# Moving the z product of a hybrid decoder layer ahead of attention, decays and the GLA preparation

## The chip, the cores and the metric

One core of one Trainium2 chip runs the whole kernel. The metric is the device time of one execution in microseconds. The runs before gave a median of 1007.89 us, from 1005.3 to 1011.02.

## What is computed

One decoder layer for 1024 tokens of width 1024, in float32. The normalized input h goes through one wide projection; its columns feed three branches, whose outputs are merged by gates and projected again.

```
h    = rms_norm(x) ; proj = h @ w_in -> aq ak av ag | gq gk gv gg gdown | sxbc sdt sz | mg
A: q,k = rope(rms_norm(aq)), rope(rms_norm(ak)); window of 128, sinks; y_a = attn(q,k,av) * silu(ag)
B: log_alpha = log_sigmoid(gdown @ w_gate_up + b) / 16, chunks of 64, cumulated inside a chunk
   y_b = rms_norm(gla(gq, gk, gv, log_alpha)) * silu(gg)
C: x,b,c = silu(causal_conv(sxbc)); dt = softplus(sdt + bias); y = ssd(x, dt, a, b, c) + D x
   y_c = group_rms_norm(y * silu(sz))
out  = x + (sum over branches of sigmoid(mg_n) * (y_n @ w_branch_n)) @ w_out
```

## The kernel before

Every large product is made of matmuls on fp32r operands, and each operand is split into a high and a low part (`wh`, `wl` for weights, `h_hi`, `h_lo` for h). `split` (L244) does it for weights: one engine rounds (ScalarE or GpSimd), another subtracts (VectorE or GpSimd), and three matmuls take the place of one. The split weights live in the pool tag `w2`, ten buffers of 128x512, which nearly all products share; raw weights come in through three buffers (`wraw`). Of the eight accumulation banks four belong to the dense products (`psd1`), four to everything else (`psm`, tag `m`).

The products with tokens on partitions are the k/v block (`kv_tiles`), two query chunks of 256 columns (`dense_tm`, called with C_Q and C_Q+1), z (`dense_pair_tm` with C_SZ) and the GLA values (C_GV). z and the values use Strassen's scheme, seven products p1 to p7 in place of eight, on sums of blocks of h: `t1`, `t2`, `t3` (`block_sums`, L487) and `t4n` (L746), all made on VectorE with help from GpSimd and ScalarE. The products with columns on partitions (`pair_fm`) use the same scheme: convolutions (`conv_pair`), merge gates (`merge_gates`), GLA q and k (`gla_pair`), branch gates `ag` and `gg`.

Written order: normalization and transposed h; k/v and first query chunk, with the rotary angles (`rope`) in between; block sums; the decays of SSD (`dz` to `acsT`, L503 to L536); the GLA preparation (L539 to L602: a small product, log-sigmoid, a cumulated sum made of 32 scans of 63 or 64 elements, and exponentials stored to `eq_d`); second query chunk; attention in eight blocks of 128 tokens; `t4n`; z; values; gates and convolutions; SSD in eight blocks; `gla_pair` and GLA in eight blocks; remaining gates; branch products (`gated`, L1054); output product.

This order is a priority and not the order of execution: when the program is built, a list scheduler with a simulated timeline fixes an order for each engine and each DMA queue, taking the instruction first in the text among those that are ready. On the chip every engine then runs its list in that fixed order. Pools are memory: a pool that is opened later may take the addresses of one that was closed before, and its first writers wait for the last users of those addresses. `glp` (GLA preparation), `att` (attention), `ssd` and `gla` follow one another in this way.

Of the kernel before, what the change touches and what calls it, by code (L numbers as in the profile page):

```python
# [26 lines left out]
NST, NW2, NHF = 4, 10, 2  # L27
# [54 lines left out]
def kernel(  # L82
# [175 lines left out]
    def dense_tm(c, evac, between=None, halves=(0, 1)):  # L258
        parts = []
        for kh in range(2):  # L260
            raw = wq.pop(0) if wq else load_w(w_tm[2 * c + kh], D, f"tm{c}_{kh}")
            parts += [split(raw[:, i * 512 : (i + 1) * 512], 512, f"tm{c}_{kh}_{i}") for i in range(2)]
        for hf in halves:
            for jj in range(2):
# [77 lines left out]
    def dense_pair_tm(c, evac, name):  # L342
# [835 lines left out]
```

## Time and profile before

| | us |
|---|---|
| median of 3 runs | 1007.89 |
| lowest and highest run | 1005.3, 1011.02 |
| profiled execution | 1011.36 |
| its span, first to last instruction | 1009.5 |
| TensorE (PE) busy | 952.8 (94%) |
| VectorE (DVE) busy | 753.0 (75%) |
| GpSimd (POOL) busy | 504.2 (50%) |
| ScalarE (ACT) busy | 446.3 (44%) |

The profile is of one execution; its times are in microseconds from the first instruction. Matmuls are pipelined and overlap in the records, so that the distance from start to start, not the length of one, is what a matmul costs. An idle time is put down to what released it. The granted clock is TensorE's, as a share of 2.4 GHz.

### The profile page before, as it was taken

What the parts mean: (1) busy time and instruction counts of PE and PEld (TensorE: products, weight loads), DVE (VectorE), ACT (ScalarE), POOL (GpSimd) and SP (SyncE); (2) the same over time, 40 slices, a digit from 0 to 9 for tenths busy, and PEclk for the clock granted to TensorE, in tenths of its full rate; (3) what the DMA queues carried; (4) which work ended last, traced back from release to release, by engine and by line L of the source; (5) the groups of instructions that cost most, each with busy time, mean ns of one, the idle gap of its engine ahead of it and who ended that gap; (6) DMA issues with size and microseconds to landing.
All of it is one profiled execution on the core that took longest, in us unless ns stands there. A gap on an engine that the chain in (4) does not pass through costs nothing.

```text
span 1009.5 us, 14874 instructions
## 1 busy us (share of the span) xinstructions
PE 952.8 (94%) x5089; PEld 804.3 (80%) x5089; DVE 753.0 (75%) x1245; ACT 446.3 (44%) x1002; POOL 504.2 (50%) x453
## 2 busy tenths in 40 slices
PE   7987879999999999999999999999899989997998
PEld 7987868898778778877888888887688878885786
DVE  4999799688799998887777554766757754589644
ACT  5433444555566467654555434444334311133221
POOL 8743557665664553344657544353344000256776
PEclk8997879899999999999999999999999999999999
DMA  9402135232324232346665444336544866763443
GB/s 370 150 32 75 54 107 183 70 120 85 110 79 129 76 118 76 116 156 212 210 181 179 136 149 135 122 119 211 187 153 173 270 211 202 247 213 107 165 148 114
DMA packets 84410, 150.14 MB, mean 149 GB/s; under 512 B 7328, under 2 KB 40304, under 8 KB 84336
## 3 DMA queue, kind: packets, MB, share of 16 engines
q1 hardware_dynamic: 84160, 149.18, 44.6%
q8 instruction: 40, 0.66, 0.3%
q14 instruction: 34, 0.28, 0.1%
q10 hardware_dynamic: 176, 0.02, 0.0%
HBM read 101.96 MB, written 47.22 MB: 148 GB/s over the span
## 4 chain that ended last, share of the span: by engine, by line
PE 53%; DVE 20%; issue 8%; DMA 7%; POOL 6%; ACT 4%; POOLq 0%; SPq 0%; DVEq 0%; ACTq 0%
PE ps_p_mg L286 16%; PE ps_u L1065 7%; PE ps_p_cv L286 5%; PE ps_p_o L286 5%; PE ps_p_gg L286 3%; PE ps_p_gqk L286 2%; PE ps_p_ag L286 2%; PE ps_tm L273 2%; PE ppv L726 1%; PE ps_kv L423 1%; DMA ybg_d<-ggy 1%; DMA e<-acs_dram 1%; PE pT L716 1%; PE ps_p_gv L369 1%; DMA el<-eq_d 1%
## 5 line engine op out<-in xcount | busy, mean ns | idle before, releaser
L286 PE MATMUL ps_p_mg<-ht_hi,wl_p_mg 128*128 128x512 f32 x192 | 75.5, 394 | 0.7 <-DVE wl_p_mg L251 0.7
L286 PE MATMUL ps_p_mg<-ht_hi,wh_p_mg 128*128 128x512 f32 x192 | 76.2, 397 | 0.0
L286 PE MATMUL ps_p_mg<-ht_lo,wh_p_mg 128*128 128x512 f32 x192 | 75.8, 395 | 0.0
L306 DVE TENSOR_TENSOR c_mg<-ps_p_mg,c_mg 128x512 f32<-128x512 f32 x84 | 56.4, 682 | 12.2 <-PE ps_p_mg L286 11.0
L251 POOL TENSOR_TENSOR wl_u<-wr_u,wh_u 128x512 fp32r<-128x512 f32 x8 | 10.6, 1328 | 100.8 <-ACT wh_u L248 100.7
L286 PE MATMUL ps_p_mg<-h_hi,wh_p_mg 128*128 128x512 f32 x144 | 56.9, 395 | 0.0
L286 PE MATMUL ps_p_mg<-h_lo,wh_p_mg 128*128 128x512 f32 x144 | 56.8, 395 | 0.0
L286 PE MATMUL ps_p_mg<-h_hi,wl_p_mg 128*128 128x512 f32 x144 | 56.5, 394 | 0.0
L251 POOL TENSOR_TENSOR wl_p_mg<-s_mg,wh_p_mg 128x512 fp32r<-128x512 f32 x24 | 31.8, 1325 | 41.4 <-ACT wh_p_mg L248 40.9
L1068 DVE SCALAR_TENSOR_TENSOR tg<-tg,ps_u 128x512 f32<-128x512 f32 x48 | 31.8, 680 | 24.9 <-DMA tg<-tg_d 22.1
L248 ACT CAST wh_p_mg<-s_mg 128x512 fp32r<-128x512 f32 x48 | 29.5, 615 | 46.7 <-POOL s_mg L298 23.6
L786 DVE SCALAR_TENSOR_TENSOR acc<-c_cv,cwh,acc 128x512 f32<-128x512 f32 (+3 forms) x48 | 40.0, 856 | 4.2 <-ACT acc L783 4.1
L286 PEld LDWEIGHTS ps_p_mg<-ht_hi,wl_p_mg 128*128 128x128 f32 x192 | 36.1, 188 | 8.2 <-DVE wl_p_mg L251 1.2
L286 PEld LDWEIGHTS ps_p_mg<-ht_hi,wh_p_mg 128*128 128x128 f32 x192 | 36.1, 188 | 7.2
L286 PEld LDWEIGHTS ps_p_mg<-ht_lo,wh_p_mg 128*128 128x128 f32 x192 | 36.1, 188 | 7.0
L251 DVE TENSOR_TENSOR wl_p_mg<-wr_mg,wh_p_mg 128x512 fp32r<-128x512 f32 x36 | 29.9, 832 | 14.3 <-PE ps_p_mg L286 6.1
L701 ACT ACTIVATE sc<-sc,nm 128x256 f32<-128x256 f32 (+1 forms) x64 | 30.8, 483 | 21.9 <-DVE nm L696 21.9
L273 PE MATMUL ps_tm<-wh_tm,h_hi 128*128 128x256 f32 x128 | 36.8, 289 | 3.9 <-ACT spl L433 3.9
L248 ACT CAST wh_u<-wr_u 128x512 fp32r<-128x512 f32 x24 | 14.9, 621 | 57.8 <-PE ps_u L1065 49.1
L308 DVE SCALAR_TENSOR_TENSOR c_o<-ps_p_o,c_o 128x512 f32<-128x512 f32 x28 | 18.9, 688 | 27.9 <-POOL c_o L312 17.6
L273 PE MATMUL ps_tm<-wl_tm,h_hi 128*128 128x256 f32 x128 | 36.3, 292 | 0.3 <-DVE wl_tm L251 0.3
L273 PE MATMUL ps_tm<-wh_tm,h_lo 128*128 128x256 f32 x128 | 36.5, 287 | 0.0
(470 smaller groups left out, 3452.2 us busy)
## 6 DMA issues: line engine op xcount, KB each, us to landing
wr_mg<-in_w_fm_dram SPq DMA_DIRECT2D x24, 512.0 KB, 3.6
tg_d<-c_mg SPq DMA_DIRECT2D x24, 512.0 KB, 2.6
tg<-tg_d SPq DMA_DIRECT2D x24, 512.0 KB, 4.4
wr_u<-in_w_br_dram SPq DMA_DIRECT2D x24, 256.0 KB, 3.5
xq<-in_xf_dram SPq DMA_DIRECT2D x8, 512.0 KB, 10.8
wr_cv<-in_w_fm_dram SPq DMA_DIRECT2D x8, 512.0 KB, 3.6
xbc_d<-acc SPq DMA_DIRECT2D x16, 256.0 KB, 2.5
e<-acs_dram SPq DMA_DIRECT2D x16, 256.0 KB, 4.9
```

The lines of the kernel that those rows point to most:

```text
L248: A.copy(hi[:, :n], raw)
L251: (lo_eng or V).tensor_tensor(out=lo[:, :n], in0=raw, in1=hi[:, :n].bitcast(F32), op=ALU.subtract)
L273: T.matmul(ps[:, j, :], lhsT=l, rhs=w, start=n == 0, stop=n == 23)
L286: T.matmul(ps, lhsT=l[:, k, :], rhs=r, start=n == 0, stop=n == 3 * kt - 1)
L306: V.tensor_tensor(out=o, in0=p, in1=c, op=op)
L308: V.scalar_tensor_tensor(out=o, in0=p, scalar=scale, in1=c, op0=ALU.mult, op1=op)
L369: T.matmul(ps[:, 256 * j : 256 * j + 256], lhsT=l, rhs=r, start=n == 0, stop=n == 11)
L423: T.matmul(ps[:, :N_KV], lhsT=l, rhs=w[:, k, :], start=n == 0, stop=n == 23)
L701: A.activation(out=sc[:, j, :nk], in_=sc[:, j, :nk], func=AF.Exp, bias=nm[:, h : h + 1], accum_out=dn[:, h : h + 1])
L786: V.scalar_tensor_tensor(out=acc[:, z:], in0=r[:, o + z - d : o + 512 - d], scalar=cwh[:, 4 * c + 3 - d : 4 * c + 4 - d], in1=acc[:, z:], ...
L1065: T.matmul(ps, lhsT=l[:, k, :], rhs=r, start=m_ == 0, stop=m_ == 11)
L1068: V.scalar_tensor_tensor(out=o, in0=o, scalar=1.0, in1=ps, op0=ALU.add, op1=ALU.mult)
```

## The change

The head: the root of a token tile's mean square goes ahead of the scaling of x by the norm's weights on GpSimd, and for the first two tiles VectorE does this scaling together with that by the root, eight times 128x128 in place of twice 128x512. Two of the four k/v weight splits change from GpSimd to VectorE or back. The high parts of the first query chunk's weights are made on ScalarE and not on GpSimd.

The second query chunk comes directly behind the first one and runs over the contraction index first (`dense_tm_by_k`): its eight token tiles accumulate side by side in the four `m` banks, and it holds only the weights of the step at hand. Its copies out come at the end.

The rotary angles go behind the block sums. `t4n` and z come next, and z's split weights get a pool of twelve buffers, `zp`, which is closed behind z; attention's pools are opened behind that. Then come the decays, whose small tiles now lie in one `w2` buffer, and attention.

The GLA preparation goes behind the last convolution, ahead of SSD. Its data is kept in an order with the halves of all chunks together, so that 4 scans of 511 or 512 elements with a row of ones and zeros that starts them anew take the place of 32; ScalarE's ReLU takes the place of VectorE's minimum; the step behind the scans is done in halves. One pair of merge gates goes ahead of `gla_pair(0)` and one ahead of `gla_pair(1)`.

```diff
--- before.py
+++ after.py
@@
-NST, NW2, NHF = 4, 10, 2
+NST, NW2, NHF, NZ = 4, 10, 2, 12
...
+    root = {}
+
     def stats(a, b):
         for t in range(a, b):
             A.activation(out=xr[t], in_=xr[t], func=AF.Square, accum_out=ssx[:, t : t + 1])
+        root[a] = rsqrt(const, rstd[:, a:b], ssx[:, a:b], b - a, 1.0 / D, EPS, f"x{a}")
+        for t in range(max(a, 2), b):
             for i in range(2):
                 hs = slice(4 * i, 4 * i + 4)
-                G.tensor_tensor(out=xs[t][:, hs], in0=xs[t][:, hs], in1=ngk[:, hs].unsqueeze(2).to_broadcast([P, 4, P]), op=ALU.mult)
-        rsqrt(const, rstd[:, a:b], ssx[:, a:b], b - a, 1.0 / D, EPS, f"x{a}")
+                with tc.issue_after(root[a].ins):
+                    G.tensor_tensor(out=xs[t][:, hs], in0=xs[t][:, hs], in1=ngk[:, hs].unsqueeze(2).to_broadcast([P, 4, P]), op=ALU.mult)
 
     def transposed(t):
         pt = mtile(f"rT{t}")
@@ -222,7 +226,11 @@
         sl = slice((t % 4) * P, (t % 4 + 1) * P)
         for kh in range(2):
             xk = xs[t][:, 4 * kh : 4 * kh + 4]
-            V.tensor_tensor(out=xk, in0=xk, in1=pt[:, :P].unsqueeze(1).to_broadcast([P, 4, P]), op=ALU.mult)
+            if t >= 2:
+                V.tensor_tensor(out=xk, in0=xk, in1=pt[:, :P].unsqueeze(1).to_broadcast([P, 4, P]), op=ALU.mult)
+            else:
+                for k in range(4 * kh, 4 * kh + 4):
+                    V.scalar_tensor_tensor(out=xs[t][:, k], in0=xs[t][:, k], scalar=ngk[:, k : k + 1], in1=pt[:, :P], op0=ALU.mult, op1=ALU.mult)
             hi, lo = (p[:, :, sl] for p in hb["12"[kh] + "12"[t // 4]])
             A.copy(hi, xk)
             V.tensor_tensor(out=lo, in0=xk, in1=hi.bitcast(F32), op=ALU.subtract)
@@ -230,9 +238,13 @@
     def split_kv(i):
         sl = slice(2 * i, 2 * i + 2)
         A.copy(wkh[:, sl], wkr[:, sl])
-        (V if i == 3 else G).tensor_tensor(out=wkl[:, sl], in0=wkr[:, sl], in1=wkh[:, sl].bitcast(F32), op=ALU.subtract)
-
-    for a in "s01 t0 w0 w1 s12 t1 w2 w3 s23 t2 s34 t3 s46 t4 t5 s68 t6 t7".split():
+        if i < 2:
+            V.tensor_tensor(out=wkl[:, sl], in0=wkr[:, sl], in1=wkh[:, sl].bitcast(F32), op=ALU.subtract)
+        else:
+            with tc.issue_after(root[1].ins):
+                G.tensor_tensor(out=wkl[:, sl], in0=wkr[:, sl], in1=wkh[:, sl].bitcast(F32), op=ALU.subtract)
+
+    for a in "s01 t0 w0 w1 s12 w2 w3 t1 s23 t2 s34 t3 s46 t4 t5 s68 t6 t7".split():
...
@@
-    def split(raw, n, name, act=False, lo_eng=None):
-        hi = wpool.tile([P, 512], F32R, tag="w2", bufs=NW2, name=f"wh_{name}")
-        lo = wpool.tile([P, 512], F32R, tag="w2", bufs=NW2, name=f"wl_{name}")
+    def work(dt, name):
+        return wpool.tile([P, 512], dt, tag="w2", bufs=NW2, name=name)
+
+    def split(raw, n, name, act=False, lo_eng=None, work=work):
+        hi, lo = work(F32R, f"wh_{name}"), work(F32R, f"wl_{name}")
...
@@
-            parts += [split(raw[:, i * 512 : (i + 1) * 512], 512, f"tm{c}_{kh}_{i}") for i in range(2)]
+            parts += [split(raw[:, i * 512 : (i + 1) * 512], 512, f"tm{c}_{kh}_{i}", act=c == C_Q) for i in range(2)]
...
@@
+    def dense_tm_by_k(c, evac):
+
+
+        raws = [load_w(w_tm[2 * c + kh], D, f"tm{c}_{kh}") for kh in range(2)]
+        banks = [psm.tile([P, 2, 256], F32, tag="m", name=f"ps_tm{c}_{b}") for b in range(4)]
+        for q in range(4):
+            parts = [p.rearrange("p (k c) -> p k c", c=256) for p in split(raws[q // 2][:, (q % 2) * 512 : (q % 2) * 512 + 512], 512, f"tm{c}_{q}", True)]
+            for k in (2 * q, 2 * q + 1):
+                hi, lo = (p[:, k % 2, :] for p in parts)
+                for b in range(4):
+                    for j in range(2):
+                        sl = slice((2 * (b % 2) + j) * P, (2 * (b % 2) + j + 1) * P)
+                        l_hi, l_lo = (r[:, sl] for r in rows_of(k, b // 2))
+                        for i, (l, w) in enumerate(((l_hi, hi), (l_lo, hi), (l_hi, lo))):
+
+                            T.matmul(banks[b][:, j, :], lhsT=l, rhs=w, start=k == 0 and i == 0 and j == 0, stop=k == KT - 1 and i == 2,
+                                     skip_group_check=True)
+        for b in range(4):
+            evac(b // 2, b % 2, banks[b])
...
@@
-    dense_tm(C_Q, spill_tm(qkv_d, 0), lambda i: [kv_tiles(q) for q in KVO[i + 1]] + ([rope()] if i == 2 else []))
+    dense_tm(C_Q, spill_tm(qkv_d, 0), lambda i: [kv_tiles(q) for q in KVO[i + 1]])
     kvp_scope.close()
+    dense_tm_by_k(C_Q + 1, spill_tm(qkv_d, 256))
...
@@
+    posf = const.tile([P, NT], F32, name="posf")
+    V.tensor_copy(posf, posi)
+    ra, rb = (st_tile(f"rope{i}", (P, 4, NT, 32)) for i in range(2))
+    ang, a2, pr, rr, fs = ra[:, 0], ra[:, 1], ra[:, 2], ra[:, 3], rb[:, 0]
...
+    hb["t4n"] = (big_tile(F32R, "ht4_hi"), big_tile(F32R, "ht4_lo"))
+    with tc.high_priority():
+        for k in range(4):
+            f1, f2 = half_tile(f"fc{k}"), half_tile(f"fd{k}")
+            whole(f1, "t2", k, G)
+            whole(f2, "21", k, V)
+            block_diff(f1, f2, f1, "t4n", k)
+
+    def z_block(col, tok, blk):
+        for i in range(2):
+            th = half_tile(f"zth{col}{tok}{i}")
+            A.activation(out=th, in_=blk[i], func=AF.Tanh, scale=0.5)
+            V.scalar_tensor_tensor(out=blk[i], in0=th, scalar=1.0, in1=blk[i], op0=ALU.add, op1=ALU.mult)
+        store_tm(z_d, col, tok, blk)
+
+    with tc.tile_pool(name="zp", bufs=NZ) as zp:
+        dense_pair_tm(C_SZ, z_block, "z", lambda dt, nm: zp.tile([P, 512], dt, tag="z2", name=nm))
...
-    with tc.tile_pool(name="smp", bufs=1) as smp:
-        dz = smp.tile([P, NT, 8], F32, name="dz")
...
+    sd = wpool.tile([P, 512], F32, tag="w2", bufs=NW2, name="sd")
+    dz, da, de, dw, dl = (sd[:, 64 * i : 64 * i + 64].rearrange("p (t h) -> p t h", h=8) for i in range(5))
+    ah, acsT = sd[:, 320:328], sd[:64, 384:512]
...
-    with tc.tile_pool(name="glp", bufs=1) as gp:
...
-            for t in range(NT):
-                o = t * P
-                V.tensor_tensor_scan(out=mn[:, f, o : o + 63][:, ::-1], data0=ones.to_broadcast([P, 63]), data1=la[:, f, o + 1 : o + 64][:, ::-1],
-                                     initial=0.0, op0=ALU.mult, op1=ALU.subtract)
-                V.tensor_tensor_scan(out=mn[:, f, o + 64 : o + P], data0=ones.to_broadcast([P, 64]), data1=la[:, f, o + 64 : o + P],
-                                     initial=0.0, op0=ALU.mult, op1=ALU.add)
...
-    dense_tm(C_Q + 1, spill_tm(qkv_d, 256))
...
-    dense_pair_tm(C_SZ, z_block, "z")
...
@@
     conv_pair(2)
+
+
+    eq_d = dram.tile([2, 2, P, S], F32, name="eq_d")
+    bmid = dcyp.tile([P, 2, NT], F32, name="bmid")
+    cst = dcyp.tile([P, 2, NT], F32, name="cst")
+    with tc.tile_pool(name="glp", bufs=1) as gp:
...
+        keep = gp.tile([P, 512], F32, name="keep")
+        G.memset(keep, 1.0)
+        G.memset(keep.rearrange("p (t l) -> p t l", l=64)[:, :, 0:1], 0.0)
...
+                A.activation(out=by_half(la, f)[:, :, ts], in_=pv, func=AF.Abs, bias=gb)
+                A.activation(out=by_half(mn, f)[:, :, ts], in_=pv, func=AF.Relu, scale=-1.0, bias=ngb[:, f : f + 1])
...
+            V.tensor_tensor_scan(out=mn[:, f, 0:511][:, ::-1], data0=keep[:, 0:511], data1=la[:, f, 1:512][:, ::-1],
+                                 initial=0.0, op0=ALU.mult, op1=ALU.subtract)
+            V.tensor_tensor_scan(out=mn[:, f, 512:S], data0=keep, data1=la[:, f, 512:S], initial=0.0, op0=ALU.mult, op1=ALU.add)
+            bv, lv = by_half(mn, f), by_half(la, f)
+            V.memset(bv[:, 0, :, 63], 0.0)
+            for h in range(2):
+                V.scalar_tensor_tensor(out=bv[:, h], in0=iot[:, 64 * h : 64 * h + 64].unsqueeze(1).to_broadcast([P, NT, 64]), scalar=av, in1=bv[:, h], op0=ALU.mult, op1=ALU.add)
+            V.scalar_tensor_tensor(out=bmid[:, f, :], in0=lv[:, 0, :, 0], scalar=av, in1=bv[:, 0, :, 0], op0=ALU.add, op1=ALU.subtract)
+            V.tensor_copy(cst[:, f, :], bv[:, 1, :, 63])
+            for i, ex in enumerate((la[:, f], eb)):
+                A.activation(out=ex.rearrange("p (t h l) -> p h t l", h=2, l=64), in_=bv, func=AF.Exp, scale=(1.0 if i == 0 else -1.0) / 16)
+                Q.dma_start(eq_d[i, f], ex)
...
@@
+    merge_gates(0, U_MGA, 0)
     gla_pair(0)
-    merge_gates(0, U_MGA, 0)
-
+    merge_gates(0, U_MGA, 2)
     gla_pair(1)
...
@@
-    merge_gates(0, U_MGA, 2)
     merge_gates(0, U_MGA, 4)
     merge_gates(0, U_MGA, 6)
```

## Rows read from the trace of the kernel before

**Rows 1.** Stages: width; busy (count) PE, PEld, DVE, ACT, POOL; clock, DMA, GB/s.

```profile
12.00:28.50 16.50, 12.27 (x55) 11.48 (x56) 11.67 (x15) 6.20 (x12) 15.58 (x18) 0.69 1.02 407
...
71.50:109.00 37.50, 26.80 (x203) 26.08 (x204) 29.55 (x59) 21.10 (x31) 8.25 (x9) 0.86 0.20 65
109.00:171.50 62.50, 48.87 (x348) 46.86 (x348) 59.87 (x100) 24.64 (x41) 43.18 (x37) 0.86 0.33 112
171.50:228.00 56.50, 53.31 (x422) 51.27 (x421) 43.58 (x98) 29.49 (x82) 36.36 (x37) 0.94 0.35 111
228.00:440.00 212.00, 209.67 (x1074) 165.07 (x1073) 188.70 (x376) 127.89 (x305) 105.25 (x96) 1.00 0.29 93
...
593.00:686.00 93.00, 93.00 (x500) 76.67 (x499) 52.11 (x82) 42.44 (x128) 40.85 (x44) 1.00 0.43 142
```

**Rows 2.** Timeline of TensorE, first query chunk: start, length, engine, line.

```profile
44.09 0.28 PE L273 MATMUL ps_tm<-wh_tm,h_hi 128*128 128x256 f32 x1
44.21 0.28 PE L273 MATMUL ps_tm<-wh_tm,h_lo 128*128 128x256 f32 x1
```

**Rows 3.** Waits of TensorE, 71.5 to 228 us: total, times, longest.

```profile
PE pacs L528 <- DVE da L526: 6.4, 1, 6.4
PE ps_p_z L369 <- ACT wh_p_z L248: 6.2, 3, 4.6
PE ps_tm L273 <- ACT spl L433: 3.9, 1, 3.9
PE ps_p_z L369 <- DVE wl_p_z L251: 3.7, 1, 3.7
```

**Rows 4.** Groups of VectorE, 92.5 to 145 us: busy us, mean ns, idle before.

```profile
L590 DVE TENSOR_TENSOR_SCAN mn<-ones,la 128x64 f32<-128x64 f32 x16 | 7.4, 462 | 0.0
L588 DVE TENSOR_TENSOR_SCAN mn<-ones,la 128x63 f32<-128x63 f32 x16 | 7.3, 459 | 0.0
L582 DVE SCALAR_TENSOR_TENSOR la<-mn,la 128x1024 f32<-128x1024 f32 x2 | 4.5, 2285 | 5.2 <-ACT la L580 5.2
...
L585 DVE TENSOR_SCALAR la<-la,avr 128x1024 f32<-128x1024 f32 x2 | 2.8, 1424 | 0.0
```

**Rows 5.** Timelines: VectorE's first step of the GLA preparation; SP's issues.

```profile
93.38 1.28 DVE L556 COPY gd<-gdT 16x512 f32<-16x512 f32 x2 [0.64 <-DMA acs_dram<-acsT]
...
140.53 0.32 SPq L600 DMA_DIRECT2D eq_d<-mn  x1
143.71 0.32 SPq L620 DMA_DIRECT2D qk<-qkv_d  x1
```

**Rows 6.** Timeline of TensorE: ends and starts along the chain.

```profile
438.77 1.09 PE L726 MATMUL ppv<-pT,vv 128*64 128x256 f32 x8
...
463.74 0.66 PE L849 MATMUL px<-ident,xin 128*128 128x128 f32 x4 [1.18 <-DMA xin<-xbc_d]
...
685.12 0.60 PE L939 MATMUL ybT<-ident,ug 128*128 128x128 f32 x4
...
740.74 0.39 PE L286 MATMUL ps_p_gg<-h_hi,wh_p_gg 128*128 128x512 f32 x1
740.96 0.39 PE L286 MATMUL ps_p_gg<-h_lo,wh_p_gg 128*128 128x512 f32 x1
```

**Rows 7.** Waits of TensorE, 9 to 28.5 us.

```profile
PE ps_kv L423 <- DVE h_lo L228: 2.9, 2, 1.8
PE rT L219 <- POOL rstd L129: 0.9, 1, 0.9
```

**Rows 8.** Timelines: VectorE's scans at 120 us, and GpSimd beside them.

```profile
120.47 0.25 DVE L588 TENSOR_TENSOR_SCAN mn<-ones,la 128x63 f32<-128x63 f32 x1
120.65 1.36 DVE L590 TENSOR_TENSOR_SCAN mn<-ones,la 128x64 f32<-128x64 f32 x1
...
120.57 5.05 POOL L351 TENSOR_TENSOR wr_a_z<-wr_a_z 128x512 f32<-128x512 f32 x4 [2.05 <-DMA wr_a_z<-in_w_tm_dram]
```

More of the change, by code (lines that the diff above doesn't have):

```diff
@@ L340, in dense_pair, with dense_pair_tm @@
         return c1, c2
-    def dense_pair_tm(c, evac, name):
+    def dense_pair_tm(c, evac, name, work=work):
         def load(i, nm):
@@ L356, in mul @@
         def mul(w, key, nm):
-            parts = [split(w[i], 512, f"{nm}{i}_{name}", True, G if nm in (Z_LO if c == C_SZ else GV_LO) else None) for i in range(2)]
+            parts = [split(w[i], 512, f"{nm}{i}_{name}", True, G if nm in (Z_LO if c == C_SZ else GV_LO) else None, work) for i in range(2)]
             out = []
@@ L388, in dense_pair_tm @@
         a22 = load(3, "a22")
-        s3 = combs([wpool.tile([P, 512], F32, tag="w2", bufs=NW2, name=f"s3{i}_{name}") for i in range(2)], a11, a21, ALU.subtract)
+        s3 = combs([work(F32, f"s3{i}_{name}") for i in range(2)], a11, a21, ALU.subtract)
         s1 = combs(a21, a21, a22, ALU.add)
@@ new lines, with frac @@
+    V.tensor_scalar(out=a1, in0=ang, scalar1=1.0, scalar2=0.0, op0=ALU.mult, op1=ALU.add)
+    V.tensor_tensor(out=a2, in0=ang, in1=a1.bitcast(F32), op=ALU.subtract)
+    def frac(v):
+        V.tensor_scalar(out=rr, in0=v, scalar1=MAGIC_ROUND, scalar2=MAGIC_ROUND, op0=ALU.add, op1=ALU.subtract)
+        V.tensor_tensor(out=v, in0=v, in1=rr, op=ALU.subtract)
+    first = True
+    for a, i in ((a2, 3), (a1, 4), (a2, 2), (a1, 3), (a2, 1), (a1, 2), (a2, 0), (a1, 1), (a1, 0)):
+        av = a.bitcast(F32) if a is a1 else a
+        tgt = fs if first else pr
+        V.tensor_scalar(out=tgt, in0=av, scalar1=C2PI[i], scalar2=None, op0=ALU.mult)
+        frac(tgt)
+        if a is a1 and i == 0:
+            frac(tgt)
+        if not first:
+            V.tensor_tensor(out=fs, in0=fs, in1=pr, op=ALU.add)
+        first = False
@@ new lines, with store_tm @@
+    V.tensor_scalar(out=pr, in0=fs, scalar1=0.25, scalar2=None, op0=ALU.add)
+    for v, dst in ((fs, 1), (pr, 0)):
+        frac(v)
+        V.tensor_scalar(out=v, in0=v, scalar1=0.49999997, scalar2=-0.49999997, op0=ALU.min, op1=ALU.max)
+        A.activation(out=cs[:, dst], in_=v, func=AF.Sin, scale=6.2831855)
+    z_d = dram.tile([NT, P, 512], F32, name="z_d")
+    gv_d = dram.tile([NT, P, 512], F32, name="gv_d")
+    def store_tm(dst, col, tok, blk):
+        for i in range(2):
+            t = 4 * tok + 2 * i
+            Q.dma_start(dst[t : t + 2, :, 256 * col : 256 * col + 256].rearrange("t p c -> p t c"), blk[i].rearrange("p (t c) -> p t c", c=256))
@@ new lines @@
+    hb["t4n"] = (big_tile(F32R, "ht4_hi"), big_tile(F32R, "ht4_lo"))
[6 more added lines that the diff above has]
+    def z_block(col, tok, blk):
+        for i in range(2):
+            th = half_tile(f"zth{col}{tok}{i}")
+            A.activation(out=th, in_=blk[i], func=AF.Tanh, scale=0.5)
+            V.scalar_tensor_tensor(out=blk[i], in0=th, scalar=1.0, in1=blk[i], op0=ALU.add, op1=ALU.mult)
+        store_tm(z_d, col, tok, blk)
@@ new lines @@
+    V.scalar_tensor_tensor(out=da, in0=dt_t, scalar=-1.0, in1=ah.unsqueeze(1).to_broadcast([P, NT, 8]), op0=ALU.mult, op1=ALU.mult)
+    pa = mtile("pacs")
+    T.matmul(pa[:, :64], lhsT=triu, rhs=da.rearrange("p t h -> p (t h)"), start=True, stop=True)
+    V.tensor_copy(acs_t.rearrange("p t h -> p (t h)"), pa[:, :64])
+    A.activation(out=eacs_t, in_=acs_t, func=AF.Exp)
+    V.tensor_single_scalar(out=nacs, in_=acs_t, scalar=-1.0, op=ALU.mult)
+    pb = mtile("pacsT")
+    T.transpose(pb[:64, :P], acs_t.rearrange("p t h -> p (t h)"), ident)
@@ L607 @@
+    V.tensor_copy(acsT, pb[:64, :P])
+    Q.dma_start(acs_dram, acsT)
     ya_d = dram.tile([P, 4, S], F32, name="ya_d")
```

196 lines of the change are left out of this document (63 added, 133 removed).

## Prediction

> **What bounds the kernel now.** I read the stage table first, cutting the span where the matmul stages change. From 228 us on TensorE is full: 209.67 us busy of the 212 to 440, 93.00 of the 93 from 593 to 686 [rows 1]. Little can be won there except by taking matmuls away, and the change takes none away. Ahead of 228 it is another picture. A 128x256 matmul starts every 0.12 us when nothing waits [rows 2]. The second query chunk's stage, 71.5 to 109, holds 188 such matmuls of 203 (22.6 us) and about 2.5 us of small ones, but lasts 37.5: 12.4 lost. The z stage, 109 to 171.5, holds 336 (40.3 us) and 1 us of attention, and lasts 62.5: 21 lost. The value stage, to 228, holds 336 again and about 9 us of attention in 56.5: 7 lost. That is 40 us, part of it idle time and part matmuls at half speed: the granted clock of these stages is 0.86, 0.86 and 0.94, so in some slices it fell from 2.4 to 1.2 GHz behind the idle stretches, and is 1.00 in the two later ones [rows 1].
>
> The list of waits says who is late: VectorE's `da` (the decays) 6.4 us, ScalarE's and VectorE's parts of z's weights 6.2 and 3.7, an evacuation 3.9 [rows 3]. VectorE is the engine behind all of them: in the z stage it is busy 59.87 of 62.5 us [rows 1], and what it does there is mostly not z: the gate angles (the GLA preparation), whose scans take 7.4 + 7.3 us and two passes 4.5 + 2.8 [rows 4]. So TensorE bounds the kernel, but ahead of 228 it is starved by VectorE's order of work.
>
> Behind that stands a chain which TensorE's fullness hides: attention (first load 143.7, last product 440), SSD (first transpose 463.7), GLA (last transpose 685.7), then the gg product from 740.7 on and the 269 us from there to the end [rows 5, 6]. Between GLA's end and gg lie 55 us of other matmuls, the slack of this chain.
>
> **The parts of the change.**
>
> Second query chunk by k in four banks. Before, its weights found no work buffers until the first chunk let go of eight of ten, and were queued on VectorE behind block sums, angles and decays; hence the 3.9 + 6.4 us and half clock after them. Now a step needs two buffers and has 48 matmuls (5.8 us at 0.12) of cover for the next split. Four evacuations come together at the end, but z accumulates in the other four banks, so they cost TensorE nothing; without that cover the price is that of the wait for an evacuation above, 3.9. I count 11 of the 12.4 us as won (bounds 6 and 12.4).
>
> z ahead, with twelve buffers of its own. The GLA preparation leaves this stretch: its four largest rows alone are 22.0 us of VectorE time [rows 4], of the 89.4 us that VectorE works between 71.5 and 171.5 [rows 1]. That leaves 67.4 us, in which decays, attention's first preparation and the smaller steps of the GLA preparation are still counted; these go behind z too, and the two products need 63 us of TensorE (22.6 + 40.3). So VectorE fits, not loosely: the angles of the rotary positions stay ahead of z in the text, now behind the block sums, and part of their work comes into this stretch. z's last weight block is loaded through SP behind others, and the t4n sums share two half tiles with the evacuations: I leave 6 us of loss. Gain 15 of 21 (bounds 5 and 20).
>
> The value product then starts near 133 instead of 171. It still shares VectorE with attention's preparation: 3 of 7 us (bounds 0 and 6).
>
> Head. TensorE waits 2.9 us for split rows of x and 0.9 us for a root on GpSimd [rows 7], and the clock is at 0.69 in those 16.5 us [rows 1]: idle 4.2, and up to 5.1 us of capacity in the clock. Roots now go ahead of the scalings on GpSimd, and two tiles' scalings (2 each) go into VectorE as eight 128x128 operations; none such is in the rows; the nearest are the 64-element scan at 0.25 us [rows 8] and an eighth of a 1024-element pass, at 2.285 / 8 = 0.29 for 128 elements [rows 4], so 2.0 to 2.3 us a tile in place of two products of 512, which by the same pass are 1.1 each. VectorE gains nothing, GpSimd is relieved. ScalarE, busy 6.20 of 16.5 us, takes casts from GpSimd free of charge. I take a gain of 4 (bounds 0 and 8).
>
> Sum of the gains: 11 + 15 + 3 + 4 = 33 us (bounds 11 and 46).
>
> The GLA preparation at its new place, behind the last convolution, ahead of SSD. It issues the same matmuls, 4 scans in place of 32, two halves instead of one pass, ReLU on ScalarE for a pass on VectorE, the same four 512 KB stores on SP. A scan of 512 lies between 0.25 us (fixed cost alone) and 8 x 0.25 = 2.0 (all by the element); the 1024-element passes grow with size, so nearer the upper: 1.4, four of them 5.6 for what was 14.7. VectorE time falls by some 9 us in all.
>
> TensorE has cover there: merge and gqk products, 18.5 us a pair (84 matmuls of 512 columns, one every 0.22 us [rows 6]). What is not free is the chain: the preparation's memory is what attention gives up, and SSD's is what the preparation gives up. Memory is given on like this in the trace: the last store of the angles issues at 140.53 and attention's first load only at 143.71 [rows 5], long after its data were there. So the preparation goes into the chain. It took 47 us before (93.38 to 140.53 [rows 5]) beside a full VectorE; from attention's end to SSD's first transpose there are 24 us now [rows 6]. I take 52 in place of these 24 (bounds 30, if SSD's loads and the preparation overlap, and 71, if they don't and it takes 47 again).
>
> The chain after is then: attention's start S + 296 (143.7 to 439.9) + 52 + 222 (463.7 to 685.7) + 3 + 269 = S + 842. With z's memory free at 133 to 135, 977 us. By TensorE: 1009.5 - 33 = 976.5. Two bounds that meet cost a little on either side, which I put at 2: span 979. The profiled execution's time is 1011.36 for a span of 1009.5, so 981; it was 3.5 us above the median of 1007.89. I predict 980, between 981 and the 977 that the median's basis would give. Half a per cent, 5 us, is about what a measurement here can tell from nothing.
>
> **The rivals.**
>
> A, the chain outlasts the filler. For it: both bounds stand at 977, so every microsecond of a longer preparation shows; VectorE is 188.70 of 212 us busy just ahead of its new place [rows 1], and SP carries the gates' weights behind its four stores. Against: the scans are fewer, and the merge gates don't need the chain. With 70 us in place of 52 the chain ends at 135 + 860 = 995, time 996; 988 to 1001 for 62 to 74.
>
> B, z still starves, by GpSimd. While GpSimd's weight sums ran (four in 5.05 us), a scan took 1.36 us instead of 0.25 [rows 8]: VectorE waits for it. z's own buffers let more of that work run early, beside VectorE's two-input operations. SBUF — State Buffer of the Trainium skill ("SBUF: two separate sides") says that a GpSimd operation and a VectorE operation with two SBUF inputs lock one pair of ports against each other for a whole instruction; the trace agrees, with 1.36 against 0.25. If VectorE so gives back 6 of the chunk's 12.4 us, 11 of z's 21 and none of the value stage's, the gain is 6 + 11 + 0 + 4 = 21 us: 988.5 by TensorE, and by the chain, with S 9 us later at 144, 986. Time 984 to 996.
>
> C, slower: attention gets z's memory too late. Nothing decides but S: at 167.5 the chain gives 1009.5, at 172 half a per cent more. If z ends at 171.5 as today, because the angles and the t4n sums stand ahead of it on VectorE, attention starts 28 us later than now and the chain ends at 1013.5 or above: 1013 to 1020. Against: at least 22 us of VectorE time leave the stretch ahead of that point.
>
> D, nothing to measure: the same with S from 161 to 171, 1003 to 1013.
>
> **How the numbers follow.** Forecast 0.58 (966 to 988; of it 0.03 lie below 966), A 0.17, B 0.13, C 0.06, D 0.06. The range 966 to 998 holds the forecast's 0.55, B, and four fifths of A: 0.82. Faster by over 0.5% (below 1002.9) are forecast, A and B: 0.88; same 0.06; slower 0.06. The forecast's own range is 966 to 988.
>
> **What would show it.** z's first matmul near 92 and its last near 133; no wait of TensorE above 4 us between 60 and 175, and a granted clock of 1.00 there; attention's first load at 130 to 140. The GLA stores at 455 to 480, SSD's first transpose at 470 to 485, GLA's last transpose near 700, and gg following within 20 us. Wrong would be: angles on VectorE between z's weight halves with TensorE idle (B, C), or idle TensorE between 440 and 740, where there is almost none today (A).

## The result, and the profile after

The changed kernel takes 996.1 us (median of four runs, 994.7 to 996.9) against 1008.7 for the kernel before on the same chip: ratio 0.9876, interval 0.9845 to 0.9908. On another chip it was 998.7 against 1008.4, ratio 0.9893 (0.9873 to 0.9913). So it is faster by 10 to 13 us, where the forecast was 28. The profiled execution took 995.85 us for a span of 994.1, 15.4 us less than the span before; the accounts below are made against these spans. The profiled execution before (1011.36) lies 2.7 us above its median, so the two traces show some 3 us more than the medians do.

The stage table of the changed kernel, cut where its matmul stages change: second query chunk, z, value product, rest of attention, attention's end to SSD's first transpose, SSD and GLA. Columns as in [rows 1].

```profile
64.10:92.10 28.00, 24.88 (x194) 24.47 (x193) 27.45 (x43) 12.03 (x20) 14.05 (x11) 0.94 0.24 81
92.10:147.70 55.60, 46.76 (x341) 45.72 (x339) 45.22 (x68) 17.50 (x30) 26.78 (x18) 0.88 0.28 93
147.70:201.40 53.70, 51.17 (x413) 49.51 (x412) 41.89 (x99) 23.85 (x66) 37.47 (x48) 0.97 0.33 107
201.40:442.60 241.20, 235.11 (x1199) 187.25 (x1198) 209.17 (x413) 145.59 (x342) 117.02 (x104) 0.99 0.30 100
442.60:502.70 60.10, 56.38 (x248) 45.36 (x247) 44.40 (x64) 31.15 (x47) 25.60 (x22) 1.00 0.38 130
502.70:732.00 229.30, 224.52 (x1190) 187.16 (x1191) 170.66 (x244) 113.79 (x324) 120.24 (x118) 1.00 0.54 174
```

Beside [rows 1]: up to the second chunk the kernel now needs 64.1 us instead of 71.5, the chunk 28.0 instead of 37.5, z 55.6 instead of 62.5, the value product 53.7 instead of 56.5. That is 26.6 us less. From there to the end it needs 792.7 instead of 781.5, 11.2 more. Some 4 of these are matmuls that moved behind the value product (the preparation's 12, 1.8 us by their starts, and 20 of attention's transposes, 2.0); about 7 are new loss. By the prediction's own measure (length less matmuls at 0.12 us and the small ones) the chunk still loses 5.0 us (12.4 before), z 15.2 (21), the value product some 5.5 (7).

TensorE's waits between 60 and 205 us, total, times, longest, to set beside [rows 3]:

```profile
PE ps_p_z L403 <- POOL wl_p_z L265: 3.5, 2, 2.7
PE ps_tm L308 <- ACT wh_tm L262: 2.4, 1, 2.4
PE ps_p_z L403 <- DVE ht_lo L487: 2.3, 1, 2.3
PE ps_p_z L403 <- ACT ht_hi L486: 2.0, 1, 2.0
...
PE ps_p_z L403 <- ACT c_z L418: 1.1, 1, 1.1
```

The decays' 6.4 us and the evacuation's 3.9 are gone. z's own waits add up to 8.9 us; the other 6.3 of its 15.2 go with the clock, granted at 0.88 over the stage (the 0.12 that it lacks are 6.7 of 55.6 us). What stands behind these waits, on the timelines of VectorE, ScalarE and GpSimd (`spl` is a copy of the second query chunk out of an accumulation bank; it and the t4n sums `fc` and `fd` share the two half tiles, buffers of 128x512):

```profile
103.61 0.29 DVE L534 TENSOR_SCALAR rope<-rope 128x256 f32<-128x256 f32 x1
104.97 0.69 DVE L467 COPY spl<-ps_tm 128x512 f32<-128x512 f32 x1 [1.07 <-DMA qkv_d<-spl]
107.90 1.33 DVE L481 TENSOR_TENSOR fd<-h_hi,h_lo 128x512 f32<-128x512 f32 x1 [2.25 <-DMA qkv_d<-spl]
...
102.94 0.42 ACT L535 ACTIVATE cs<-rope 128x256 f32<-128x256 f32 x1 [10.89 <-DVE rope L534]
103.27 0.57 ACT L467 COPY spl<-ps_tm 128x512 f32<-128x512 f32 x1
...
106.21 1.26 POOL L481 TENSOR_TENSOR fc<-ht_hi,ht_lo 128x512 f32<-128x512 f32 x1 [15.76 <-DMA qkv_d<-spl]
107.43 1.26 POOL L265 TENSOR_TENSOR wl_p_z<-wr_a_z,wh_p_z 128x512 fp32r<-128x512 f32 x1
```

Read from the bottom: GpSimd's `wl_p_z`, for which TensorE waits, stands behind the first t4n sum `fc`; that idled 15.76 us for a half tile, which a copy out of the second chunk (`spl`) held; and the copies stood on VectorE behind the block of rotary angles, and on ScalarE behind Sin, which waits for the same angles.

The block of angles and decays is itself drawn out. VectorE and GpSimd ahead of the stretch above:

```profile
83.66 0.21 DVE L581 TENSOR_TENSOR sd<-sd 128x64 f32<-128x64 f32 x1
83.99 1.31 DVE L582 TENSOR_TENSOR sd<-sd 128x64 f32<-128x64 f32 x1
...
83.92 5.11 POOL L385 TENSOR_TENSOR wr_a_z<-wr_a_z 128x512 f32<-128x512 f32 x4 [0.46 <-DVE sd L581]
```

Between 78 and 91 us, while GpSimd makes weight sums and halves for z, nine small operations of VectorE (four of the angles, five of the decays) take 0.90 to 1.53 us each; the same shapes take 0.20 to 0.43 where GpSimd is idle. That is some 9.5 us of the block that ends at 103.9, an estimate from these durations. This is rival B's mechanism.

The chain, answering [rows 5] and [rows 6], from timelines of SP, TensorE and VectorE:

```profile
147.75 0.33 SPq L609 DMA_DIRECT2D qk<-qkv_d  x1
...
441.54 1.09 PE L715 MATMUL ppv<-pT,vv 128*64 128x256 f32 x8
...
446.11 1.28 DVE L788 COPY eb<-gdT 16x512 f32<-16x512 f32 x2 [1.52 <-DMA ya_d<-yat]
...
491.03 0.32 SPq L842 DMA_DIRECT2D eq_d<-eb  x1
...
502.73 0.63 PE L888 MATMUL px<-ident,xin 128*128 128x128 f32 x4 [1.42 <-DMA e<-acs_dram]
...
726.54 0.39 PE L320 MATMUL ps_p_gg<-h_hi,wh_p_gg 128*128 128x512 f32 x1
...
731.30 0.60 PE L979 MATMUL ybT<-ident,ug 128*128 128x128 f32 x4
```

Attention's first load comes at 147.75, later than before (143.71); the preparation takes 45 us; SSD's first transpose comes 60 us after attention's end, where I had 52. The gg product begins 5 us ahead of GLA's last transpose. In the head, [rows 7] has given way to two waits between 9 and 28.5 us, and the clock granted from 12 to 28.5 is 1.00 instead of 0.69:

```profile
PE ps_kv L457 <- ACT h_hi L235: 1.7, 1, 1.7
PE ps_tm L287 <- ACT wh_tm L262: 0.5, 1, 0.5
```

### The profile page after: what moved, and what is told of

Same layout as the page of the kernel before. It is cut to its first block, busy times and chain, and to the rows that moved or that the text cites. A ratio compares the mean times of both kernels' runs of the same rounds, so it can differ in the third digit from the quotient of the medians.

```text
span 994.1 us, 14844 instructions
## 1 busy us (share of the span) xinstructions
PE 944.2 (95%) x5089; PEld 795.8 (80%) x5089; DVE 765.0 (77%) x1228; ACT 451.1 (45%) x1014; POOL 491.2 (49%) x442
## 4 chain that ended last, share of the span: by engine, by line
PE 40%; DVE 12%; DMA 8%; issue 7%; POOL 5%; ACT 5%; SPq 0%; POOLq 0%; DVEq 0%; ACTq 0%
PE ps_p_mg L320 14%; PE ps_p_o L320 5%; PE ps_p_ag L320 4%; PE ps_u L1104 3%; PE ps_p_cv L320 3%; DMA tg<-tg_d 2%; PE ps_p_gqk L320 2%; DVE acc L749 1%; DMA tl<-t_d 1%; DMA yc_r<-yc_d 1%; PE py L928 1%; PE ppv L715 1%; DMA yb_r<-ybg_d 1%; POOL s_o L332 1%; PE psc L677 1%
## 5 line engine op out<-in xcount | busy, mean ns | idle before, releaser
L265 POOL TENSOR_TENSOR wl_u<-wr_u,wh_u 128x512 fp32r<-128x512 f32 x8 | 10.6, 1331 | 98.6 <-ACT wh_u L262 98.5
L320 PE MATMUL ps_p_mg<-h_hi,wh_p_mg 128*128 128x512 f32 x144 | 56.5, 392 | 0.0
L265 DVE TENSOR_TENSOR wl_p_mg<-wr_mg,wh_p_mg 128x512 fp32r<-128x512 f32 x36 | 38.4, 1074 | 15.7 <-ACT wh_p_mg L262 8.9
L733 ACT ACTIVATE c_mg<-c_mg 128x1024 f32<-128x1024 f32 x24 | 25.4, 1056 | 15.3 <-DVE c_mg L340 12.5
L320 PEld LDWEIGHTS ps_p_mg<-h_lo,wh_p_mg 128*128 128x128 f32 x144 | 27.1, 188 | 5.4
L320 PEld LDWEIGHTS ps_p_mg<-h_hi,wl_p_mg 128*128 128x128 f32 x144 | 27.1, 188 | 5.3
```

Of the source, the lines that this page charges most:

```text
L265: (lo_eng or V).tensor_tensor(out=lo[:, :n], in0=raw, in1=hi[:, :n].bitcast(F32), op=ALU.subtract)
L320: T.matmul(ps, lhsT=l[:, k, :], rhs=r, start=n == 0, stop=n == 3 * kt - 1)
L733: A.activation(out=c, in_=c, func=AF.Tanh, scale=0.5)
```

## The experiments

Ratios are to the kernel before on the same chip, with 95% intervals; "z's last" is z's last matmul, "first product" attention's. Gains and losses against the changed kernel compare ratios with its two, 0.9876 and 0.9893. The expectations count 46 operations of VectorE for the angles; the traces have 48.

**1. Sin late.** The angles' results are written to `cs`, and Sin follows z's last tanh.

```diff
-        V.tensor_scalar(out=v, in0=v, ...)
-        A.activation(out=cs[:, dst], in_=v, func=AF.Sin, ...)
+        V.tensor_scalar(out=cs[:, dst], in0=v, ...)
...
+    with tc.issue_after(zlast[0].ins):
+        for dst in range(2):
+            A.activation(out=cs[:, dst], in_=cs[:, dst], func=AF.Sin, ...)
```

> After with one edit: VectorE's chain of rotary angles stays where it is and writes its clipped values into cs; the two Sin activations follow z's last tanh on ScalarE, in place on cs. Theory 1 (ScalarE's order: Sin waits 10.89 us for VectorE, and the copies out and casts behind it wait too): z's last matmul goes from 147.7 to 139 to 142 us, the time from 996.1 to 988 to 991. Theory 2 (VectorE's chain of some 46 small operations is itself what z waits for): z's last matmul stays within 2 us, the time at 994 to 998. Theory 3 (the t4n sums find only two half tiles, which the copies out of the second chunk hold): the two copies on VectorE still stand behind its chain, so at most 3 us, 993 to 996.

1000.6 us, 0.9926 (0.9902 to 0.9950), above all three forecasts; z's last 145.7. Taking away the 10.89 us that ScalarE idles brings z 2 us and the end nothing: theory 1 falls.

**2. Half tiles of their own** for the t4n sums (`fc`, `fd` from a pool of four).

> After with one edit: the t4n sums get four half tiles of their own, in a pool that lives as long as z's. Theory 3 (half tiles): GpSimd's first t4n sum moves from 106.2 us to before 92, its idle 15.76 us go, z's last matmul comes at 137 to 141, time 986 to 990. Theory 1 (ScalarE's order): the copy of z's first product still comes behind Sin at 104; z ends at 144 to 147, time 993 to 996. Theory 2 (VectorE's chain): VectorE's half of the sums still stands behind the angles, z ends at 145 to 148, time 994 to 997.

998.9 us, 0.9907 (0.9883 to 0.9931). z's last comes at 141.7, 6 us earlier, but the value product's last at 201.0 (201.4 in the changed kernel). Its waits between 60 and 201 us:

```profile
PE qT L651 <- ACT qh L647: 4.3, 1, 4.3
PE ps_tm L308 <- ACT wh_tm L262: 4.2, 1, 4.2
PE ps_p_z L403 <- DVE c_z L409: 3.1, 1, 3.1
```

The half tiles held most of z's wait, and taking it away wins nothing: TensorE, which works through its list in order, now waits for attention's first transposes, for VectorE's additions behind the angles, and for weights that GpSimd's earlier sums delay (beside them VectorE's sums take 1.78 us instead of 0.68).

**3. Angles behind z.** The whole block is issued after z's last VectorE operation.

> After with one edit: the whole block of rotary angles is ordered behind z's last VectorE operation. All three theories of z's wait want z to end earlier here, theory 2 most: z's last matmul at 133 to 138 instead of 147.7 (theory 1 and 3: 137 to 142). The angles, 46 operations at about 0.32 us, then lie ahead of attention's first rotation: attention's first product stays within 5 us of 190.7. If the chain from attention to the gates sets the end as much as TensorE does, the time stays at 993 to 998 in spite of z's gain; if only TensorE's fullness sets it, it falls to 984 to 988.

1014.5 us, 1.0053 (1.0034 to 1.0073). Its z stage and SSD's first transpose:

```profile
91.50:134.40 42.90, 40.72 (x338) 40.30 (x336) 31.49 (x35) 13.45 (x23) 19.95 (x13) 1.00 0.32 108
...
518.55 1.09 PE L892 MATMUL px<-ident,xin 128*128 128x128 f32 x4 [7.71 <-DMA bcin<-xbc_d]
```

z runs at full clock almost without loss. Attention's first product comes at 219.0, 28 us late, not within 5 as forecast, and TensorE then runs dry ahead of SSD: from 440 to 620 us it is busy for 167.0 us at a clock of 0.93 (171.5 at 1.00 in the changed kernel). When it is this late, the chain does bind.

**4. Angles early**, inside the first query chunk as in the kernel before.

> After with one edit: the angles stand where they stood in the kernel before, in the first query chunk behind its third bank. Theory 2 (VectorE is full, the angles only move the wait): z's first matmul comes 5 to 12 us later than 92.1 and the time is within 3 us of 996. Theory 1 and 3 (place in the order, not sum): z's first matmul within 3 us of 92, its last at 137 to 142, attention begins earlier by as much, time 986 to 990.

999.0 us, 0.9913 (0.9884 to 0.9943): z's first matmul of the main run at 95.0, z's last at 147.5; a wait of 5.7 us for VectorE's `wl_tm` opens in the second chunk. The wait moves and the time is within 3 us, as theory 2 has it, though z's first matmul is 3 us late and not 5 to 12.

**5. No angles.**

```diff
-    posf = const.tile([P, NT], F32, name="posf")
...
-        A.activation(out=cs[:, dst], in_=v, func=AF.Sin, scale=6.2831855)
+    G.memset(cs, 0.5)
```

> After with the rotary angles left out: cs is filled with a constant on GpSimd, the 46 VectorE operations and two Sin go. Theory A (VectorE's sum of work up to attention's first product sets z's end and attention's start together, and what it gains there reaches the end): z's last matmul at 134 to 137 us instead of 147.7, attention's first product at 176 to 182 instead of 190.7, time 980 to 986. Theory B (what z gains is given back behind it whatever VectorE does, the end being set by what comes after attention): z at 134 to 137, time 990 to 998.

988.4 us, 0.9801 (0.9770 to 0.9832). The z stage and the value stage:

```profile
93.70:135.70 42.00, 40.76 (x341) 40.55 (x339) 33.38 (x37) 15.57 (x27) 28.34 (x18) 1.00 0.38 121
135.70:192.70 57.00, 53.09 (x412) 51.45 (x411) 41.89 (x99) 23.49 (x65) 37.71 (x48) 0.91 0.31 100
```

The stage is 13.6 us shorter than in the changed kernel and z loses next to nothing (42.0 us for 40.3 of matmuls); the value stage gives back 3.3, with 3.9 us of waits for attention's first transposes and a clock of 0.91; 7.5 to 9.5 reach the end. Without the angles z's loss is gone; the size lies between both theories.

**6. Angles in the head**, where VectorE idles, with loads and buffers of their own.

> After with the angles moved to where VectorE idles (6.35 us ahead of its first weight split at 8.5, 3.46 us at 28.7): positions and row constants are loaded first on ScalarE's queue, the angles have a buffer of their own and are written behind the head, Sin follows the last cast of x. Theory A: z's last matmul at 135 to 140, attention's first product at 177 to 184; the head loses 2 to 4 us; time 983 to 990. Theory B: 992 to 998. If the idle time of the head is not usable, the kv product starts later by up to 10 us and the time is 994 to 1001.

1005.7 us, 0.9974 (0.9955 to 0.9992), above all three forecasts. VectorE and GpSimd around the start of its z product (window 92 to 120, then GpSimd's timeline):

```profile
92.00:120.00 28.00, 24.52 (x197) 24.32 (x197) 7.74 (x13) 9.73 (x17) 15.87 (x13) 0.95 0.17 57
...
97.02 2.63 POOL L300 TENSOR_TENSOR wl_p_z<-wr_a_z,wh_p_z 128x512 fp32r<-128x512 f32 x2 [18.50 <-ACT wh_p_z L297]
...
114.89 1.26 POOL L516 TENSOR_TENSOR fc<-ht_hi,ht_lo 128x512 f32<-128x512 f32 x1 [5.52 <-DMA qkv_d<-spl]
```

The head and the first chunk end 6 us later. VectorE is busy 7.74 of 28 us and z still takes 53.5: ScalarE casts weights late and copies out behind them, and the half tiles are late again. The same wait has another engine behind it, so an idle VectorE alone is not enough.

**7. GLA preparation ahead of attention** (its new form, behind z and the decays).

> After with the GLA preparation (in its new form) put back ahead of attention, behind z and the decays. From attention's end to SSD's first transpose: 20 to 35 us instead of 60. Theory A: VectorE's sum ahead of attention grows by the preparation, attention's first product comes 20 to 35 us later than 190.7, and the time is 1005 to 1018. Theory B (the end is set by the stretch from attention's end to SSD): that stretch falls by 30 us or so and pays for the later start: 990 to 998.

1016.0 us, 1.0073 (1.0051 to 1.0096). Attention's first product comes at 261.1, 70 us later, more than expected; from attention's end (512.1) to SSD's first transpose (522.7) only 10.6 us are left, and that pays for little of it. The time is theory A's.

**8. Head alone**, on the kernel before.

> Before with the head part of the change alone (order of roots, scalings and weight splits, casts of the first query chunk on ScalarE). If what the head gains reaches the end, 6 to 7 us less than before by the stage accounts of the two traces (my forecast for this part was 4): 1001 to 1003. If VectorE's later waits take it back: 1006 to 1009.

1010.3 us, 1.0017 (1.0003 to 1.0031). Its waits between 60 and 170 us:

```profile
PE ps_p_z L381 <- ACT wh_p_z L260: 13.7, 4, 8.3
PE pacs L540 <- DVE da L538: 7.2, 1, 7.2
```

It is ahead by 7 us at 60 us. z takes part of this, where 6.2 us for `wh_p_z` have become 13.7, and ends 3.6 us ahead (167.9 against 171.5); but the value product is 11 us ahead again, and all of it is gone by GLA's last transpose (685.12 before):

```profile
216.97 0.28 PE L381 MATMUL ps_p_gv<-wl_p_gv,h_hi 128*128 128x256 f32 x1
...
686.57 0.60 PE L951 MATMUL ybT<-ident,ug 128*128 128x128 f32 x4
```

So the lead is lost in attention and SSD, by several short waits, and not in z alone; which edit of the order causes them was not tried. (Of the four k/v splits three change their engine, not two as said above.)

**9. Angles spread** behind VectorE's last copy out, Sin behind z.

> After with one edit in the order of VectorE and ScalarE: the angles are ordered behind VectorE's last copy out of the second query chunk (and so run between the t4n sums and z's additions), and Sin behind z's last tanh. Theory C (the order: 46 small operations in one block ahead of the copies out and of the t4n sums, while VectorE idles some 10 us of z's stage later on): z's last matmul at 136 to 141 us instead of 147.7, attention's first product at 181 to 187 instead of 190.7, time 987 to 992, near the 988.4 without angles. Theory D (the sum: the angles' 15 us of VectorE have to be paid ahead of attention wherever they stand): z may end earlier, attention's first product stays at 188 to 193, time 994 to 999.

1007.1 us, 0.9979 (0.9954 to 1.0004). VectorE is full throughout z's stage:

```profile
92.00:120.00 28.00, 22.75 (x187) 22.34 (x186) 27.55 (x46) 10.61 (x18) 16.56 (x12) 0.99 0.12 38
120.00:148.00 28.00, 17.92 (x109) 17.11 (x110) 27.45 (x46) 5.76 (x11) 13.28 (x9) 0.80 0.30 96
```

z's last comes at 152.9 and the first product at 203.4, worse than either theory: theory C falls. VectorE idled ahead of 92 us here (busy 12.2 of the 28 us from 64 on, 27.5 in the changed kernel) and paid for it in the stage.

**10. Parts undone in the changed kernel**: the head; the second chunk half by half; z in the shared buffers.

> After with the head of before (order of roots, scalings and splits, casts of the first query chunk on GpSimd). If the gains of the parts add up, the head's 5 to 7 us are lost: 1001 to 1003. If a later wait for VectorE takes up what the head gains, as in before with the new head alone (1010.3 against 1009.1): 994 to 998.

> After with the second query chunk as in before: half by half, all eight weight buffers ahead of the first matmul. If the gains of the parts add up, the 8 to 11 us of this part are lost: 1004 to 1007. If VectorE's order behind it sets the pace, z's first matmul comes later by 5 to 12 us but z's last within 3 us of 147.7, and the time is 994 to 999.

> After with z's work tiles taken from the ten shared ones instead of twelve of its own. If z's own buffers carry its gain (z's weights split ahead, 15 us in my forecast), z's last matmul comes 5 to 12 us later than 147.7 and the time is 1001 to 1008. If they are idle weight because VectorE's order is what z waits for: within 3 us of 147.7, 994 to 999; attention's memory is then free earlier, and its first load no longer waits for z.

Without the head 1005.2 us, 0.9967 (0.9950 to 0.9984): 7.5 to 9 us lost, more than either forecast. With the old chunk 1003.4 us, 0.9945 (0.9926 to 0.9964): 5 to 7 lost. With shared buffers 1000.2 us, 0.9902 (0.9872 to 0.9932): 1 to 2.5 more, within what the intervals can tell, although attention's first load comes at 97.0, its first product at 181.9 and SSD's first transpose at 485.5, 17 us earlier than in the changed kernel.

**11. Short angles.** 24 operations instead of 48.

```diff
-    for a, i in ((a2, 3), (a1, 4), (a2, 2), (a1, 3), (a2, 1), (a1, 2), (a2, 0), (a1, 1), (a1, 0)):
+    for a, i in ((a2, 1), (a1, 2), (a2, 0), (a1, 1), (a1, 0)):
...
-        frac(tgt)
         if a is a1 and i == 0:
+            frac(tgt)
             frac(tgt)
```

> After with the angles' chain cut from 46 VectorE operations to 24 at the same place: for positions below 5120 the four smallest products lie below single precision and only the largest needs its whole turns taken out. If the price of the angles is that of VectorE's work (7.7 us reached the end for 46 operations and two Sin), about half of it: z's last matmul at 140 to 143 us instead of 147.7, time 990 to 994. If it is the place in the order that costs, the block ends 7 us earlier and the wait goes with it: z at 136 to 139, time 988 to 990. If it was only the different order of that build: 995 to 999.

> After with the short angles and the t4n sums' own half tiles together. If the two half tiles are the next thing that z waits for once the angles are shorter: 3 to 5 us better than short angles alone, 985 to 989. If attention's first preparation takes it back, as with the half tiles alone (z's last matmul 6 us earlier, the value product's no earlier): within 2 us of short angles alone.

> After once more, beside the short angles on the same chip, since their intervals against before overlap (0.9876 from 0.9845 to 0.9908, and 0.9844 from 0.9821 to 0.9866). If the 3.6 us between the two medians are the angles' work, after is at 0.987 to 0.989 of before here; if they are scatter between chips, the two ratios lie within 0.001 of each other.

> The short angles once more, beside after. By work saved (22 operations of VectorE ahead of attention): 0.983 to 0.985 of before, 3 to 5 us below after. If scatter: within 0.001 of after's ratio.

992.5 us, 0.9844 (0.9821 to 0.9866), z's last at 142.3, attention's first product at 185.1: about half of what leaving the angles out wins. With the t4n sums' own half tiles 993.0 us, 0.9850 (0.9825 to 0.9875): z's last at 138.1, the value product's at 195.1 against 195.8, nothing more. Beside the changed kernel on one chip: 992.8 us, 0.9831 (0.9803 to 0.9859), and 998.7 us, 0.9893 (0.9873 to 0.9913). The short angles beat both kernels; VectorE's operations on the angles take 12.4 us in place of 21.2.

**12. No preparation, and the move alone** (the latter on the kernel before).

> After with the GLA preparation's arithmetic left out at its new place: the four stores write a constant, the 8 transposes and 4 products and everything on VectorE and ScalarE go. If the stretch from attention's end to SSD's first transpose binds (52 us in my sum, 60 measured): that stretch falls to 30 or less and the time to 980 to 986. If TensorE's full order binds and only its own waits count (2.0 us for the preparation, 1.4 us for SSD's first load): SSD's first transpose comes earlier, but the time is 990 to 994.

> Before with one part of the change alone: the GLA preparation, in its new form, moved behind the last convolution. After with that part undone took 1016.0, 20 us more than after. If the move is what wins and the other parts add little without it: 992 to 1002. If it wins only together with z ahead and the new second query chunk: 1003 to 1009.

Without the arithmetic 989.2 us, 0.9818 (0.9793 to 0.9842). SSD's first transpose and GLA's last, and TensorE from 440 to 620 us:

```profile
456.48 0.60 PE L828 MATMUL px<-ident,xin 128*128 128x128 f32 x4
...
678.68 0.60 PE L919 MATMUL ybT<-ident,ug 128*128 128x128 f32 x4
...
440.00:620.00 180.00, 176.19 (x917) 146.67 (x916) 125.03 (x182) 85.99 (x232) 100.92 (x97) 1.00 0.57 186
```

The same window of the changed kernel:

```profile
440.00:620.00 180.00, 171.53 (x858) 141.38 (x857) 137.26 (x196) 96.33 (x225) 94.29 (x89) 1.00 0.53 173
```

The chain ends 52.6 us earlier (731.3 to 678.7) and the time falls by 6 to 7.5. Of the 7.3 us between the two spans 4.7 are TensorE's idle time in this window, and 1.8 are the preparation's own 12 matmuls, which are gone too. The move alone: 1001.1 us, 0.9924 (0.9905 to 0.9944), so it wins some 7 by itself, although its SSD begins at 486.1 and its GLA ends at 710.7, 22 and 26 us later than before.

## Why the prediction was wrong

**The term that failed is z's: "gain 15 of 21", "I leave 6 us of loss".** z still loses 15.2. Two causes that I named for the 6 are real ones: angles ahead of z, t4n sums and evacuations on two half tiles. What I mis-sized is what they do in series: the angles hold VectorE in one block, the copies out stand behind it, the t4n sums behind the copies, GpSimd's weight halves behind the sums, and the granted clock falls to 0.88. Leaving the angles out takes away 13.6 us of z (experiment 5), halving them 3.9 (z's 51.7 against 55.6). My count of VectorE's time (67.4 us for 63) was a sum and said nothing on this order. It was short as well: VectorE works 72.7 us in the two stages and 21.0 of them on the angles, where the kernel before had 8.5 in its two. And VectorE was not behind every wait: in the kernel before, z's casts (`wh_p_z`) stood behind the preparation's own work on ScalarE, which kept it busy from 95.18 to 110.45 us.

**A term was missing.** I charged the preparation's new place to the chain alone. TensorE's waits of the changed kernel between 205 and 740 us:

```profile
PE ppv L715 <- DVE pT L709: 4.6, 2, 2.5
...
PE ps_p_gqk L320 <- DVE mn L835: 2.0, 1, 2.0
...
PE px L888 <- DMA e<-acs_dram: 1.4, 1, 1.4
```

The preparation's share is 4.7 us (experiment 12): from 440 to 620 us TensorE idles 8.5 us, 3.8 without it and 2.5 in the kernel before, by waits at gqk (2.0, for the preparation's `mn`), at SSD's first load (1.4) and in SSD. Another 3.8 us of the new loss lie in attention, where TensorE idles 6.1 of 241.2 us instead of 2.3 of 212; 4.6 of them are waits for VectorE's `pT`, which the run without the preparation has as well. What causes those was not tried.

**The other terms.** Second chunk 7.4 by the stage table and 5 to 7 by its undoing, for 11: the first step's weights come late (waits of 2.4 and 0.7 us, and a clock of 0.94 over the chunk). Value stage 1.5 for 3. Head 7.4 for 4, inside its bounds. With z's 5.8 the sum is 22 instead of 33, and less about 7 it is the 15.4 of the two spans. The time lies beyond the forecast's own range (966 to 988), and that it lies within 966 to 998 is partly luck: the head's 3.4 us more than forecast made up for a part of the rest.

**"Two bounds that meet" is wrong as it stands.** I gave the chain S + 842 = 977, S being attention's first load, and took it to bind as tightly as TensorE. SSD came 46 us earlier in experiment 12, and the time fell by about TensorE's own share (4.7 and 1.8 us); it came 17 earlier with shared buffers, where S was 97.0 and not 147.75, and the time did not fall at all; in the move alone it came 22 later than in the kernel before, and the time fell. In the other direction it does bind: 16 us later in experiment 3, the time was 16 to 18 us longer. So the chain has little slack against lateness, and earliness alone won nothing; that TensorE's order of work was fixed when the kernel was built is the likely reason, not a tested one. Of the chain's pieces attention's 296 us held (294.9, from 147.75 to 442.6); S came 12.75 us late, the stretch to SSD took 60 for 52, and SSD and GLA 229 for 222.

**The rivals.** A has the time (988 to 1001) and its sign, idle TensorE behind 440 us (8.5 us of 440 to 620, 2.5 before), but not the cause: the stretch took 60 us and not 62 to 74, and emptying it won 6 to 7.5 (experiment 12). B has z starving and a time just at its edge (996); what starved z was VectorE's and then GpSimd's order. Its mechanism is in the trace, with some 9.5 us in the block that z waits for, but no run tried it by itself: how much of z's loss it is stays open. C's mechanism, attention late, is what experiments 3 and 7 show when angles or preparation stand ahead of it. Of my signs, z's last matmul (133 forecast, 147.7), the clock (1.00, 0.88), attention's first load, the GLA stores (455 to 480, 484.8 to 491.0), SSD's first transpose (470 to 485, 502.7) and GLA's last (700, 731.3) were wrong; z's first matmul, no wait above 4 us, and gg next to GLA's end were right. The scans, estimated at 1.4 us, took 1.2:

```profile
L833 DVE TENSOR_TENSOR_SCAN mn<-keep,la 128x512 f32<-128x512 f32 x2 | 2.4, 1194 | 0.0
```

**What is shown.** VectorE's work ahead of attention's first product is paid for in the end time: leaving out the angles, shortening them, moving the preparation behind attention all win; a wait in z taken away without less work (half tiles, in both versions) is taken up by TensorE's other waits, most of all for attention's first transposes; work put between z and attention's first product (experiments 3 and 7) costs more than it saves elsewhere. The parts do not add up: the head is worth nothing in the kernel before and 7.5 to 9 in the changed one; the undoings of head, chunk, buffers and move together cost over 30 us, of a gain of 10 to 13.

**What stays open.** Each build is ordered anew by the planner, so that an edit moves other instructions by some us; why Sin late is 3 to 5 us slower than the changed kernel was not followed further. The order and the lengthened operations of VectorE were not separated: no run kept the angles and took GpSimd's sums from beside them.

## What to carry to other kernels

A stage's loss is won only as far as the next wait on the same in-order engines: name that next wait and its size before entering the gain. Work that moves is charged twice, to the chain and to the waits of the engine that is full at its new place. A part's worth is measured both ways, alone on the old kernel and undone in the new one; where the two differ, the parts do not add up, and the forecast of their sum is too sure. The cheapest gain here was less work on the engine that the others wait for (24 small operations of VectorE for 3 to 6 us).

## What the runs showed of the hardware

A GpSimd sum of two SBUF operands that takes 1.26 us in the changed kernel took 5.61 in experiment 2, beside a VectorE that ran such operations back to back, each at its usual 0.68:

```profile
74.02 5.61 POOL L481 TENSOR_TENSOR fc<-ht_hi,ht_lo 128x512 f32<-128x512 f32 x1 [4.84 <-DVE ht_lo L487]
...
75.40 0.68 DVE L487 TENSOR_TENSOR ht_lo<-fa,ht_hi 128x512 fp32r<-128x512 f32 x1
76.00 0.68 DVE L265 TENSOR_TENSOR wl_tm<-wr_tm,wh_tm 128x512 fp32r<-128x512 f32 x1
76.60 0.68 DVE L481 TENSOR_TENSOR fd<-h_hi,h_lo 128x512 f32<-128x512 f32 x1
```

SBUF — State Buffer of the Trainium skill ("SBUF: two separate sides") says that the two engines lock a shared pair of ports against each other for such operations; the trace agrees in that one of the two waits, and here it is GpSimd that pays, where in [rows 8], and in the changed kernel between 78 and 91 us, it was VectorE.
